# Three of eight column chunks of x transposed by VectorE blocks and a round trip through DRAM, in a one-core hybrid encoder layer

## The chip, the core and the metric

The kernel runs on one core of one Trainium2 chip. The core has five engines, each working through its own queue in order: TensorE (PE in the profile; its weight loads are PEld), VectorE (DVE), ScalarE (ACT), GpSimd (POOL) and SyncE (SP), which here only issues transfers. Transfers run on 16 DMA engines that all queues share. The metric is the device time of the core in microseconds (us), the median of several runs: 633.74 before the change (three runs, 633.61 to 633.91).

## The reference

One layer of a bidirectional hybrid encoder, 512 tokens by 2048 features, in float32: x is normalised, projected by w_in to q, k, v, two gates and an LRU input; attention and a gated linear recurrence run on their parts; both are normalised, gated, and projected by w_out onto x.

```python
def hybrid_layer(x, norm_w, w_in, ...):
    h = rms_norm(x, norm_w)
    proj = jnp.einsum('bsd,de->bse', h, w_in)
    q, k, v, g_attn, xr, g_lru = jnp.split(proj, SPLITS, axis=-1)
    attn_out = attention_group(q, k, v, q_norm_w, k_norm_w)
    lru_out = lru_group(xr, conv_w, conv_b, lru_wa, lru_ba, lru_wx, lru_bx, lru_lambda)
    mixed = jnp.concatenate([rms_norm(attn_out, attn_norm_w) * jax.nn.silu(g_attn),
                             rms_norm(lru_out, lru_norm_w) * jax.nn.silu(g_lru)], axis=-1)
    return x + jnp.einsum('bse,ed->bsd', mixed, w_out)
```

## The kernel before

Every matrix product is made of three products of split operands: a float32 value v is kept as a high part (v rounded to the fp32r type) and a low part (v minus the high part), and `mm3` (lines 151 to 154) multiplies high by high, low by high and high by low. So each operand costs a cast on ScalarE (the high) and a subtraction on VectorE (the low).

The program begins with the first half of the LRU input's projection, `proj_feat(C_XR, a1, ...)` (line 301): four accumulators `pj_162` to `pj_165` in PSUM, and eight chunks c = 0 to 7 of 256 input features each. Below, "x5" is chunk 5 of x and "w5" chunk 5 of w_in. For chunk c it needs

- the rows of w_in (512 KB), loaded by `wraw` into a ring of three buffers `wr`, split by `wsplit` (lines 216 and 217) into `wh` and `wl`, of which there are two chunks' worth;
- 256 columns of x for all 512 tokens (512 KB), loaded by `xload` (line 235) into a buffer `b`, with tokens on the partitions, and turned so that features lie on the partitions. `xturn` (line 238) does that on TensorE: for each half of the chunk four 128x128 transposes into PSUM (line 242), which ScalarE scales by norm_w into the high `xh` (line 244) and VectorE into the low `xl` (line 245), both named x in the profile;
- 24 matmuls (four accumulators, two halves, three products).

`xsquare` (line 249) adds up the squares of each token in the untransposed chunk. When all eight are in, `xstats` (line 293) makes 1/rms on GpSimd (`rstd`), puts it on two diagonals (line 284, `k_106` and `k_107` before, `k_109` and `k_110` after) and spreads it over the partitions by two matmuls (line 290) and a copy (`rbc`, line 291). The accumulators are multiplied by rbc when they are read out (line 395, `evac_bc`). The small vectors of the LRU (conv_w, biases, lambda, norms) are loaded in seven transfers into `vec_st` by `vec_load` (line 179), transposed once on TensorE by `columns` (line 188, the tile `mm_553` before, `mm_609` after) and copied into `vec` on VectorE (line 190). `lru_consts` (line 359) makes constants `lc` of vec in some 25 tiny VectorE steps.

What sets the order: TensorE runs in the order of the program text. SP does so until the end of this stage, ScalarE and VectorE until chunk 1's third accumulator (`s1`, `s2` in lines 1075 to 1080); after that a scheduler orders them by priority, with loads, splits and turns of x raised by `high_priority(AHEAD)`. In the compiled program each transfer of SP carries one of eight completion semaphores in turn, and waits until the transfer that had the same one before has landed.

In the last part of the program the attention already turns q and k without TensorE: `sent` (line 551) transposes 32x32 blocks on VectorE (line 559), writes the result to DRAM (`qd`, line 565), and `landed` (line 568) reads it back in four transfers that put each block in its place (`lq`, line 573); `moved` (line 643) does the same with the attention weights (`u`, `pd`, `pt`).

Of the kernel before, what the change touches and what calls it, by code (L numbers as in the profile page):

```python
# [17 lines left out]
P = 128  # L18
# [33 lines left out]
B = 32  # L52
NQ = P // B

# [8 lines left out]
def hybrid_kernel(  # L63
# [144 lines left out]
    turn_of = [0]  # L208

    def wsplit(raw, k, copy=nc.scalar.copy):  # L210
# [6 lines left out]
        nc.vector.tensor_sub(lo, raw[:, k, :], f(hi))  # L217
# [9 lines left out]
    ssq = const([P, NT, KT // 2], "ssq")  # L227

# [9 lines left out]
    def xturn(xc, kk):  # L238
# [5 lines left out]
        nc.scalar.activation(xh[kk], pt, AF.Identity, scale=nw[:, kk : kk + 1])  # L244
# [4 lines left out]
    def xsquare(xc, c):  # L249
        for t in range(NT):  # L250
            nc.vector.scalar_tensor_tensor(
                xc[:, t, :], xc[:, t, :], 1.0, xc[:, t, :], op0=ALU.mult, op1=ALU.mult,
                accum_out=ssq[:, t, c : c + 1],
            )

    def xchunk(c):
        with tc.high_priority(AHEAD):
            (xc,) = xload(c)
        yield
        with tc.high_priority(AHEAD):  # L260
            for k in range(2):
                xturn(xc, 2 * c + k)
        xsquare(xc, c)
# [287 lines left out]
    def sent(es, nh, *us):  # L551
# [5 lines left out]
        for n, u in enumerate(us):  # L557
            for t, e in enumerate(es):
                nc.vector.transpose(
                    u[:, :, :, t, :].rearrange("p b h r -> p h b r"),  # L560
                    e[:, 2 * n : 2 * n + 2].rearrange("p h (b c) -> p h b c", c=B),
                )
            aside_ = dram.tile([P, NQ, 2 * SEQ // NQ], F32, name=nm("qd"), tag="qd", bufs=5)
            yield
            nc.sync.dma_start(aside_, u.rearrange("p b h t r -> p b (h t r)"))
            asides.append(aside_)

    def landed(aside_):

        to = pools["qkv"].tile([P, NQ, 2, NT, B], F32, tag="lq", bufs=2, name=nm("lq"))  # L570
        src = aside_.rearrange("(i c) b x -> b c i x", c=B)
        for b in range(NQ):
            nc.sync.dma_start(
                to[b * B : (b + 1) * B].rearrange("p i h t r -> p i (h t r)"), src[b]
            )
        return to

    def split_head(pair, k, hi, lo):
        src = pair[:, :, k]
        hi, lo = (v.rearrange("p (t i r) -> p i t r", t=NT, i=NQ) for v in (hi, lo))  # L580
# [513 lines left out]
    loads, turns = iter(chunks), iter(chunks)  # L1094
    for step in proj_feat(C_XR, a1, first, given):
        if step is None:
# [4 lines left out]
            next(next(loads), None)  # L1101
# [232 lines left out]
```

## Time and profile before

| | |
|---|---|
| median of 3 runs | 633.74 us (633.61 to 633.91) |
| the profiled execution, its own time | 634.36 us |
| its span in the profile | 632.2 us |
| TensorE, VectorE, ScalarE, GpSimd busy | 99%, 78%, 54%, 17% of the span |
| mean DMA rate over the span | 197 GB/s |
| granted TensorE clock | 1.00 |

The profile is of one execution. Its timeline gives start and length of each instruction, with the tile it writes and those it reads; "[1.64 <-ACT x L244]" means that the engine stood idle for 1.64 us before it and that ScalarE's line 244 ended that. Matmuls are pipelined, so their lengths overlap (0.39 each) and the distance from start to start, 0.2275 in this stage, is what one costs. The other engines overlap a little too: a 128x512 subtraction on VectorE lasts 0.69 and the next starts after 0.60.

### The profile page before, as it was taken

What the parts mean: (1) busy time and instruction counts of PE and PEld (TensorE: products, weight loads), DVE (VectorE), ACT (ScalarE), POOL (GpSimd) and SP (SyncE); (2) the same over time, 40 slices, a digit from 0 to 9 for tenths busy, and PEclk for the clock granted to TensorE, in tenths of its full rate; (3) what the DMA queues carried; (4) which work ended last, traced back from release to release, by engine and by line L of the source; (5) the groups of instructions that cost most, each with busy time, mean ns of one, the idle gap of its engine ahead of it and who ended that gap; (6) DMA issues with size and microseconds to landing.
All of it is one profiled execution on the core that took longest, in us unless ns stands there. A gap on an engine that the chain in (4) does not pass through costs nothing.

```text
span 632.2 us, 8303 instructions
## 1 busy us (share of the span) xinstructions
PE 625.8 (99%) x2795; PEld 516.4 (82%) x2795; DVE 492.9 (78%) x808; ACT 341.6 (54%) x582; POOL 104.5 (17%) x137
## 2 busy tenths in 40 slices
PE   8999999999999999999999999999999999999997
PEld 6888888888888888888888888888888888888885
DVE  5789688986698875787787887549978866886885
ACT  3534799479936822645475547335445534443441
POOL 0010110212003532521123233100310001010010
PEclk9999999999999999999999999999999999999999
DMA  9844675768774599389659646923995676796152
GB/s 298 272 146 131 156 191 152 186 145 192 217 235 156 167 221 259 78 193 270 198 175 271 198 129 186 275 80 112 244 236 186 220 242 226 291 355 217 67 200 101
DMA packets 71436, 124.48 MB, mean 197 GB/s; under 512 B 6377, under 2 KB 27489, under 8 KB 71393
## 3 DMA queue, kind: packets, MB, share of 16 engines
q1 hardware_dynamic: 63360, 106.11, 53.1%
q0 software_dynamic: 7712, 17.31, 14.1%
q10 hardware_dynamic: 320, 0.53, 0.3%
q8 instruction: 22, 0.36, 0.2%
q14 instruction: 22, 0.17, 0.1%
HBM read 108.72 MB, written 36.18 MB: 229 GB/s over the span
## 4 chain that ended last, share of the span: by engine, by line
PE 98%; DMA 1%; ACT 0%; DVE 0%; ACTq 0%; DVEq 0%; issue 0%
PE pj L152 20%; PE pj L153 20%; PE pj L154 20%; PE mm L955 14%; PE pj L955 10%; PE mm L154 3%; PE mm L152 3%; PE mm L153 3%; DMA wr<-in_w_in_dram 1%; PE mm L242 1%; PE pj L310 0%; PE mm L749 0%; PE mm L290 0%; DVE cb L986 0%; ACT wh L216 0%; ACT x L244 0%
## 5 line engine op out<-in xcount | busy, mean ns | idle before, releaser
L152 PE MATMUL pj<-x,wh 128*128 128x512 f32 x376 | 147.2, 392 | 0.0
L153 PE MATMUL pj<-x,wh 128*128 128x512 f32 x376 | 146.6, 390 | 0.0
L154 PE MATMUL pj<-x,wl 128*128 128x512 f32 x376 | 146.4, 389 | 0.0
L216 ACT CAST wh<-wr 128x512 fp32r<-128x512 f32 x143 | 85.9, 618 | 104.4 <-PE pj L153 41.9
L217 DVE TENSOR_TENSOR wl<-wr,wh 128x512 fp32r<-128x512 f32 x144 | 100.4, 723 | 22.0 <-ACT wh L216 20.9
L807 ACT CAST wh<-wr 128x1024 fp32r<-128x1024 f32 (+1 forms) x72 | 60.7, 860 | 74.9 <-PE mm L955 37.7
L808 DVE TENSOR_TENSOR wl<-wr,wh 128x1024 fp32r<-128x1024 f32 (+1 forms) x72 | 68.7, 984 | 28.2 <-ACT wh L807 28.1
L153 PEld LDWEIGHTS pj<-x,wh 128*128 128x128 f32 x376 | 70.6, 188 | 14.9 <-DVE x L245 0.3
L154 PEld LDWEIGHTS pj<-x,wl 128*128 128x128 f32 x376 | 70.6, 188 | 14.9
L152 PEld LDWEIGHTS pj<-x,wh 128*128 128x128 f32 x376 | 70.6, 188 | 14.6
L152 PE MATMUL pj<-wh,x 128*128 128x512 f32 x192 | 74.8, 390 | 0.0
L154 PE MATMUL pj<-wh,x 128*128 128x512 f32 x192 | 74.7, 389 | 0.0
L153 PE MATMUL pj<-wl,x 128*128 128x512 f32 x192 | 74.7, 389 | 0.0
L831 POOL DMA_DIRECT2D t<-in_w_out_dram x40 | 33.7, 909 | 139.3 <-DMA t<-in_w_out_dram 95.5
L955 PE MATMUL mm<-wl,mh 128*128 128x512 f32 x128 | 49.8, 389 | 0.0
L955 PE MATMUL mm<-wh,ml 128*128 128x512 f32 x128 | 49.8, 389 | 0.0
L955 PE MATMUL mm<-wh,mh 128*128 128x512 f32 x128 | 49.8, 389 | 0.0
L153 PEld LDWEIGHTS pj<-wl,x 128*128 128x128 f32 x192 | 36.0, 188 | 7.5
L152 PEld LDWEIGHTS pj<-wh,x 128*128 128x128 f32 x192 | 36.0, 188 | 7.5
L154 PEld LDWEIGHTS pj<-wh,x 128*128 128x128 f32 x192 | 36.0, 188 | 7.5
L637 POOL TENSOR_SCALAR p<-p,sm 128x512 f32<-128x512 f32 x32 | 24.2, 759 | 90.2 <-DVE sm L636 90.2
L955 PE MATMUL pj<-wl,mh 128*128 128x512 f32 x96 | 37.4, 389 | 0.0
(203 smaller groups left out, 1032.1 us busy)
## 6 DMA issues: line engine op xcount, KB each, us to landing
wr<-in_w_in_dram SPq DMA_DIRECT2D x71, 512.0 KB, 4.5
wr<-in_w_out_dram SPq DMA_DIRECT2D x24, 512.0 KB, 5.1
t<-in_w_out_dram POOLq DMA_DIRECT2D x40, 256.0 KB, 7.1
wr<-t SPq DMA_DIRECT2D x40, 256.0 KB, 5.0
pd<-u SPq DMA_DIRECT2D x16, 512.0 KB, 3.4
pt<-pd SPq DMA_DIRECT2D x64, 128.0 KB, 4.0
t<-in_w_out_dram SPq DMA_DIRECT2D x24, 256.0 KB, 4.7
t<-t SPq DMA_DIRECT2D x16, 256.0 KB, 5.4
```

The costliest lines, as they stand in the source:

```text
L152: nc.tensor.matmul(acc, lh, rh, start=start, stop=False)
L153: nc.tensor.matmul(acc, lh, rl, start=False, stop=False)
L154: nc.tensor.matmul(acc, ll, rh, start=False, stop=stop)
L216: copy(hi, raw[:, k, :])
L217: nc.vector.tensor_sub(lo, raw[:, k, :], f(hi))
L242: nc.tensor.transpose(pt[:, t * P : (t + 1) * P], xc[:, t, ks], ident)
L637: last_pool[0] = nc.gpsimd.tensor_scalar(p, p, sm, 0.0, op0=ALU.mult, op1=ALU.add).ins
L807: nc.scalar.copy(hi[:, to], b)
L808: nc.vector.tensor_sub(lo[:, to], b, f(hi[:, to]))
L831: nc.gpsimd.dma_start(dst, src, accum_op=ALU.add)
L955: nc.tensor.matmul(dst[s], lh[:, ts_], rh, start=i == 0 and j == 0, stop=i == 7 and j == 2)
```

## The change

x0 to x4 are turned as before. x5, x6 and x7 (`TURNED = 5`) take another way: VectorE transposes the 32x32 blocks of the chunk in four instructions (`blocks`, into a tile `xu`), SP writes them to DRAM (`put_aside`, `xd`) and reads them back in four transfers of 128 KB that put the blocks in place (`bring_back`, into a second tile `xu`), ScalarE scales both halves by norm_w in place and casts the highs, and VectorE subtracts for the lows. So 24 transposes of TensorE, with the six scalings and six subtractions from PSUM behind them, go, and 12 block transposes, 3 writes, 12 reads, 6 scalings, 6 casts and 6 subtractions come.

The squares of x5 to x7 (12 instructions) move from VectorE to ScalarE. A table `moves` says at which accumulator step each load, split and turn is put into the program. Pins (`issue_after`) queue one instruction behind another on its engine: the blocks of x5 behind the lows of w2 and those of x6 and x7 behind those of w3, the squares behind x4's highs, the scalings behind the latest split, the statistics behind x7's last low. The loads of vec_st go from behind x5's load to behind the reads of x7, the transpose of vec_st from after chunk 5 to after chunk 6, and the loads of the rope tables (`rk`, `rq`) behind the last load of this stage.

```diff
@@ -50,6 +50,7 @@
 
 
 B = 32
+TURNED = 5
 NQ = P // B
 
 
...
@@ -205,7 +206,7 @@
             loads_done[queue] = queue.dma_start(raw[:, ks, :], src[:, ks, :]).ins
             yield raw
 
-    turn_of = [0]
+    turn_of, split_done = [0], {}
 
     def wsplit(raw, k, copy=nc.scalar.copy):
 
...
@@ -214,7 +215,8 @@
         hi = pool.tile([P, SEQ], F32R, tag="wh", bufs=4, name=nm("wh"))
         lo = pool.tile([P, SEQ], F32R, tag="wl", bufs=4, name=nm("wl"))
         copy(hi, raw[:, k, :])
-        nc.vector.tensor_sub(lo, raw[:, k, :], f(hi))
+        done = nc.vector.tensor_sub(lo, raw[:, k, :], f(hi)).ins
+        split_done[-1] = split_done[turn_of[0] - k] = done
         return hi, lo
 
     def wload(w, r0, c0):
...
@@ -225,6 +227,7 @@
 
     xh, xl = [None] * KT, [None] * KT
     ssq = const([P, NT, KT // 2], "ssq")
+    highs, x_lows = {}, []
 
     def xload(c, nk=1):
 
...
@@ -241,26 +244,84 @@
             ks = slice(kk % 2 * P, (kk % 2 + 1) * P)
             nc.tensor.transpose(pt[:, t * P : (t + 1) * P], xc[:, t, ks], ident)
         xh[kk], xl[kk] = x2(), x2()
-        nc.scalar.activation(xh[kk], pt, AF.Identity, scale=nw[:, kk : kk + 1])
+        after = split_done[-1] if kk > 3 else None
+        with tc.issue_after(after) if after else nullcontext():
+            highs[kk // 2] = nc.scalar.activation(
+                xh[kk], pt, AF.Identity, scale=nw[:, kk : kk + 1]
+            ).ins
         nc.vector.scalar_tensor_tensor(
             xl[kk], pt, nw[:, kk : kk + 1], f(xh[kk]), op0=ALU.mult, op1=ALU.subtract
         )
 
     def xsquare(xc, c):
         for t in range(NT):
+            if c >= TURNED:
+                nc.scalar.activation(
+                    xc[:, t, :], xc[:, t, :], AF.Square, accum_out=ssq[:, t, c : c + 1]
+                )
+                continue
             nc.vector.scalar_tensor_tensor(
                 xc[:, t, :], xc[:, t, :], 1.0, xc[:, t, :], op0=ALU.mult, op1=ALU.mult,
                 accum_out=ssq[:, t, c : c + 1],
             )
 
+    def blocks(u, t, src):
+
+        nc.vector.transpose(
+            u[:, :, :, t, :].rearrange("p b k r -> p k b r"),
+            src.rearrange("p (k b c) -> p k b c", k=2, c=B),
+        )
+
+    def put_aside(u, tag, bufs):
+
+        aside_ = dram.tile([P, NQ, 2 * SEQ // NQ], F32, name=nm(tag), tag=tag, bufs=bufs)
+        nc.sync.dma_start(aside_, u.rearrange("p b k t r -> p b (k t r)"))
+        return aside_
+
+    def bring_back(to, aside_):
+
+        src = aside_.rearrange("(i c) b x -> b c i x", c=B)
+        for b in range(NQ):
+            nc.sync.dma_start(
+                to[b * B : (b + 1) * B].rearrange("p i k t r -> p i (k t r)"), src[b]
+            )
+
+    def in_order(v):
+        return v.rearrange("p (t i r) -> p i t r", t=NT, i=NQ)
+
     def xchunk(c):
         with tc.high_priority(AHEAD):
             (xc,) = xload(c)
         yield
+        if c < TURNED:
+            with tc.high_priority(AHEAD):
+                for k in range(2):
+                    xturn(xc, 2 * c + k)
+            xsquare(xc, c)
+            yield
+            return
+        u, back = (
+            ring.tile([P, NQ, 2, NT, B], F32, name=nm("xu")) for ring in (aring, hring)
+        )
+        with tc.high_priority(AHEAD), tc.issue_after(split_done[2 if c == TURNED else 3]):
+            for t in range(NT):
+                blocks(u, t, xc[:, t, :])
+            there = put_aside(u, "xd", KT // 2 - TURNED)
+        with tc.issue_after(highs[TURNED - 1]):
+            xsquare(xc, c)
+        yield
         with tc.high_priority(AHEAD):
+            bring_back(back, there)
+        yield
+        with tc.high_priority(AHEAD), tc.issue_after(split_done[-1]):
             for k in range(2):
-                xturn(xc, 2 * c + k)
-        xsquare(xc, c)
+                kk = 2 * c + k
+                xh[kk], xl[kk] = x2(), x2()
+                hi, lo = (in_order(v) for v in (xh[kk], xl[kk]))
+                v = back[:, :, k]
+                nc.scalar.activation(v, v, AF.Identity, scale=nw[:, kk : kk + 1])
+                nc.scalar.copy(hi, v)
+                x_lows.append(nc.vector.tensor_sub(lo, v, f(hi)).ins)
         yield
 
     last_pool = [None]
...
@@ -494,7 +555,8 @@
     def rope_consts():
         rq, rk = (pools["rope"].tile([P, NT, 2, HD], F32, name=n, tag=n) for n in ("rq", "rk"))
         for dst, src, sc in ((rk, k_norm_w, 1.0), (rq, q_norm_w, HD**-0.5)):
-            nc.sync.dma_start(dst, rope.rearrange("(t p) c d -> p t c d", p=P))
+            with tc.issue_after(last_x):
+                nc.sync.dma_start(dst, rope.rearrange("(t p) c d -> p t c d", p=P))
             wb = k2(shape=(P, 2, HD))
             nc.sync.dma_start(wb[:, 0, :], src[None, :].broadcast_to([P, HD]))
             if sc != 1.0:
...
@@ -1091,33 +1144,58 @@
         xturn(xc, 0)
         busy(WARM2)
     chunks = [xchunk(c) for c in range(1, KT // 2)]
-    loads, turns = iter(chunks), iter(chunks)
+
+    raws = {}
+
+    def fetch_x(c):
+        with tc.high_priority(AHEAD):
+            (raws[c],) = wraw(w_in, c * 2 * P, C_XR)
+
+    def split_x(c):
+        with tc.high_priority(AHEAD):
+            given[c] = [wsplit(raws[c], k) for k in range(2)]
+
+    moves = {
+        None: "x1", (0, 2): "x1",
+        (1, 0): "x2", (1, 1): "x2", (1, 2): "x3 w2 s2", (1, 3): "x3",
+        (2, 0): "x4 x5", (2, 1): "x4 w3", (2, 2): "x6 x7", (2, 3): "w4 s3",
+        (3, 0): "x5 w5 x5", (3, 1): "x6 x7", (3, 3): "s4 x5",
+        (4, 0): "w6 x6 x7", (4, 3): "s5 x6",
+        (5, 0): "w7", (5, 3): "s6 x7", (6, 3): "s7",
+    }
+
+    def move(step):
+        for name in moves.get(step, "").split():
+            n = int(name[1])
+            if name[0] == "x":
+                next(chunks[n - 1])
+            else:
+                (fetch_x if name[0] == "w" else split_x)(n)
+
     for step in proj_feat(C_XR, a1, first, given):
         if step is None:
             with tc.high_priority():
                 first.append(wsplit(raw, 1))
                 xturn(xc, 1)
             xsquare(xc, 0)
-            next(next(loads), None)
+            move(None)
             given[1] = wload(w_in, 2 * P, C_XR)
             continue
         c, e = step
-        if (e == 0 or e == 2) and c:
-            next(next(loads, iter(())), None)
-        if (e, c) == (2, 0) or (e == 1 and c) or (e, c) in ((3, 1), (3, 2)):
-            next(next(turns, iter(())), None)
+        move(step)
         if (c, e) == (1, 2):
-            given[2] = wload(w_in, 4 * P, C_XR)
             s2.close()
-        if (c, e) == (2, 3):
-            vec_load()
-        if (c, e) == (5, 3):
+        if (c, e) == (4, 2):
+            with tc.high_priority(AHEAD):
+                vec_load()
+        if (c, e) == (6, 3):
             columns(vec, vec_st)
         if (c, e) == (KT // 2 - 1, 0):
-            with tc.high_priority():
+            with tc.high_priority(), tc.issue_after(x_lows[-1]):
                 xstats()
 
     s1.close()
+    last_x = loads_done[nc.sync]
     lru_consts()
     fill = proj_feat(C_XR + SEQ, a2)
     wsums = itertools.chain(first_sums(), more_sums())
```

The hunk left out lets `sent` and `landed` call the same new helpers; what they do is unchanged.

Three places of the compiled order, as they stand before and now. First SP, from x5's load (`b_57` before) and w4's load (`wr_380` now) on. Before:

```order
L235 DMA b_57_366<-in_x_dram 128x4x256
L179 DMA vec_st<-in_conv_w_dram 32x128
L179 DMA vec_st<-in_conv_b_dram 8x128
L179 DMA vec_st<-in_lru_ba_dram 16x128
L179 DMA vec_st<-in_lru_bx_dram 16x128
L179 DMA vec_st<-in_lru_lambda_dram 16x128
L179 DMA vec_st<-in_attn_norm_w_dram 8x128
L179 DMA vec_st<-in_lru_norm_w_dram 8x128
L205 DMA wr_403<-in_w_in_dram 128x2x512
L235 DMA b_69_419<-in_x_dram 128x4x256
L235 DMA b_76_455<-in_x_dram 128x4x256
L205 DMA wr_463<-in_w_in_dram 128x2x512
```

Now (w3, `wr_362`, x6 and x7 stand right before this, behind x5):

```order
L206 DMA wr_380<-in_w_in_dram 128x2x512
L278 DMA xd_402<-xu_396 128x1024
L206 DMA wr_408<-in_w_in_dram 128x2x512
L285 DMA xu_397<-xd_402 32x4x256 x4
L278 DMA xd_426<-xu_420 128x1024
L278 DMA xd_438<-xu_432 128x1024
L206 DMA wr_480<-in_w_in_dram 128x2x512
L285 DMA xu_421<-xd_426 32x4x256 x4
L285 DMA xu_433<-xd_438 32x4x256 x4
L180 DMA vec_st<-in_conv_w_dram 32x128
```

`wr_403` and `wr_362` are w3, `wr_463` and `wr_380` w4, `wr_408` w5, `wr_480` w6; `xd_402`, `xd_426` and `xd_438` are x5, x6 and x7 in DRAM. vec_st has moved from ahead of w3 to behind x7's reads; w7 (`wr_539`) comes right after the seventh of its loads.

Then VectorE in the middle of the stage, from the lows of w2 (`wl_288`, `wl_292`) on. Before:

```order
L217 TENSOR_TENSOR wl_288<-wr_285,wh_287 128x512
L217 TENSOR_TENSOR wl_292<-wr_285,wh_291 128x512
L245 SCALAR_TENSOR_TENSOR x_46_308<-mm_302,nw,x_45_307 128x512
L245 SCALAR_TENSOR_TENSOR x_49_317<-mm_311,nw,x_48_316 128x512
L217 TENSOR_TENSOR wl_406<-wr_403,wh_405 128x512
L217 TENSOR_TENSOR wl_410<-wr_403,wh_409 128x512
L251 SCALAR_TENSOR_TENSOR b_38_283,ssq<-b_38_283 128x256 x3
L245 SCALAR_TENSOR_TENSOR x_53_344<-mm_338,nw,x_52_343 128x512
L245 SCALAR_TENSOR_TENSOR x_56_353<-mm_347,nw,x_55_352 128x512
L251 SCALAR_TENSOR_TENSOR b_38_283,ssq<-b_38_283 128x256
```

Now:

```order
L218 TENSOR_TENSOR wl_288<-wr_285,wh_287 128x512
L218 TENSOR_TENSOR wl_292<-wr_285,wh_291 128x512
L252 SCALAR_TENSOR_TENSOR x_46_308<-mm_302,nw,x_45_307 128x512
L252 SCALAR_TENSOR_TENSOR x_49_317<-mm_311,nw,x_48_316 128x512
L218 TENSOR_TENSOR wl_383<-wr_362,wh_382 128x512
L218 TENSOR_TENSOR wl_387<-wr_362,wh_386 128x512
L270 STREAM_TRANSPOSE xu_396<-b_51_332 128x2x4x32 x3
L252 SCALAR_TENSOR_TENSOR x_54_346<-mm_340,nw,x_53_345 128x512
L252 SCALAR_TENSOR_TENSOR x_57_355<-mm_349,nw,x_56_354 128x512
L270 STREAM_TRANSPOSE xu_396<-b_51_332 128x2x4x32
```

`wl_406`, `wl_410` before and `wl_383`, `wl_387` now are the lows of w3; the pairs of line 245 (now 252) are the lows of x3 and x4. Where squares of x3 stood, the block transposes of x5 (`xu_396`) stand, and then those of x6.

Last VectorE at the end of the stage, around the copy of vec. Before:

```order
L295 TENSOR_REDUCE xsum<-ssq 128x4
L217 TENSOR_TENSOR wl_563<-wr_556,wh_562 128x512
L281 CAST part_610<-rstd 128x4
L282 TENSOR_TENSOR part_611<-rstd,part_610 128x4
L284 TENSOR_TENSOR k_106_612<-ident,part_610 128x512
L284 TENSOR_TENSOR k_107_613<-ident,part_611 128x512
L217 TENSOR_TENSOR wl_593<-wr_590,wh_592 128x512
L190 COPY vec<-mm_553 128x104
L217 TENSOR_TENSOR wl_597<-wr_590,wh_596 128x512
L364 TENSOR_SCALAR lc_641<-vec 128x16
L365 TENSOR_TENSOR lc_641<-lc_641,vec 128x16
```

Now:

```order
L356 TENSOR_REDUCE xsum<-ssq 128x4
L342 CAST part_622<-rstd 128x4
L343 TENSOR_TENSOR part_623<-rstd,part_622 128x4
L345 TENSOR_TENSOR k_109_624<-ident,part_622 128x512
L191 COPY vec<-mm_609 128x104
L345 TENSOR_TENSOR k_110_625<-ident,part_623 128x512
L425 TENSOR_SCALAR lc_653<-vec 128x16
L426 TENSOR_TENSOR lc_653<-lc_653,vec 128x16
L218 TENSOR_TENSOR wl_602<-wr_539,wh_601 128x512
L218 TENSOR_TENSOR wl_606<-wr_539,wh_605 128x512
L428 TENSOR_SCALAR lc_655<-lc_654 128x16
L438 TENSOR_SCALAR lc_653<-vec 128x16
```

`wl_593` and `wl_597` before and `wl_602` and `wl_606` now are the lows of w7. Before, they stood on both sides of the copy, and the copy's transpose `mm_553` was one chunk further ahead on TensorE. Now they stand behind the copy, the second diagonal `k_110` and two steps of `lc`. On TensorE `mm_609` stands between chunk 6's last matmul and chunk 7's first, and chunk 7's third matmul reads `wl_602`.

More of the change, by code (lines that the diff above doesn't have):

```diff
@@ L1 @@
 import itertools
-from contextlib import ExitStack
+from contextlib import ExitStack, nullcontext
 import numpy as np
@@ L558, in sent @@
             for t, e in enumerate(es):
[L559 to L563, printed above, removed]
+                blocks(u, t, e[:, 2 * n : 2 * n + 2].rearrange("p h d -> p (h d)"))
             yield
-            nc.sync.dma_start(aside_, u.rearrange("p b h t r -> p b (h t r)"))
-            asides.append(aside_)
+            asides.append(put_aside(u, "qd", 5))
     def landed(aside_):
         to = pools["qkv"].tile([P, NQ, 2, NT, B], F32, tag="lq", bufs=2, name=nm("lq"))
[L571 to L575, printed above, removed]
+        bring_back(to, aside_)
         return to
@@ L579, in split_head @@
         src = pair[:, :, k]
-        hi, lo = (v.rearrange("p (t i r) -> p i t r", t=NT, i=NQ) for v in (hi, lo))
+        hi, lo = (in_order(v) for v in (hi, lo))
         nc.scalar.copy(hi, src)
```

## The prediction

> **What bounds the kernel now.** I read the page first (part 1, then part 4, the chain that ended last), then a table of busy time by stage, then the timelines of the first 60 us, where the whole change lies.
>
> ```profile
> span 632.2 us, 8303 instructions
> PE 625.8 (99%) x2795; PEld 516.4 (82%) x2795; DVE 492.9 (78%) x808; ACT 341.6 (54%) x582; POOL 104.5 (17%) x137
> PE 98%; DMA 1%; ACT 0%; DVE 0%; ACTq 0%; DVEq 0%; issue 0%
> 12.60:60.00 47.40, 47.40 (x234) 39.38 (x233) 39.94 (x127) 19.25 (x32) 1.60 (x2) 1.00 0.59 191
> L242 PE MATMUL mm<-ident,b 128*128 128x128 f32 x64 | 8.5, 273 | 0.0
> ```
>
> TensorE is the bound, alone: 98% of the chain, and from 12.6 to 60 us it is busy for 47.40 of 47.40 us at a granted clock of 1.00. VectorE has 39.94 of the 47.40, ScalarE only 19.25. So a TensorE instruction taken out is worth its full pitch, and any new wait of TensorE costs its full length. The last row is what the change attacks: 64 transposes of x, of which chunks 5 to 7 have 24.
>
> **The gain.** Each chunk's eight transposes stand between two projection matmuls:
>
> ```profile
> 27.05 0.39 PE L154 MATMUL pj<-x,wl 128*128 128x512 f32 x1
> 27.28 1.03 PE L242 MATMUL mm<-ident,b 128*128 128x128 f32 x8
> 28.07 0.48 PE L152 MATMUL pj<-x,wh 128*128 128x512 f32 x1
> 28.38 0.40 PE L153 MATMUL pj<-x,wh 128*128 128x512 f32 x1
> ```
>
> Start to start, 27.05 to 28.38 is 1.33 us for what would be two matmul pitches of 0.2275: 0.875 us for eight transposes. Three chunks: **-2.63 us**. TensorE reaches 27.28 unchanged; without the transposes a chunk of 24 matmuls takes 24 x 0.2275 = 5.46 us, so chunk 3 starts at 27.28, chunk 5 at 38.2, chunk 6 at 43.66, and the transpose of vec_st, now ahead of chunk 7, comes at 49.12.
>
> **The new round trip, chunk 5.** Its start hangs on VectorE's queue:
>
> ```profile
> GB/s 0 230 308 376 380 352 366 358 320 41 121 274 370 261 365 369 377 274 289 12 0 0 259 50 39 351 303 232 256 19 0 187 112 5 30 336 214 34 241 183
> 18.21 1.14 ACT L216 CAST wh<-wr 128x512 fp32r<-128x512 f32 x2
> 21.65 1.14 ACT L216 CAST wh<-wr 128x512 fp32r<-128x512 f32 x2 [2.30 <-DMA wr<-in_w_in_dram]
> 20.48 1.29 DVE L217 TENSOR_TENSOR wl<-wr,wh 128x512 fp32r<-128x512 f32 x2
> 23.41 1.41 DVE L245 SCALAR_TENSOR_TENSOR x<-mm,nw,x 128x512 fp32r<-128x512 f32 x2 [1.64 <-ACT x L244]
> 227.63 2.07 DVE L559 STREAM_TRANSPOSE uq<-ev 128x256 f32<-128x256 f32 x6
> ```
>
> The first row (40 slices of the first 70 us) shows the DMA engines full to 15.75 us and nearly still after. The seven vec_st loads now leave, w3, x6, x7 and w4 follow x5 at once, and at 0.52 MB over 360 GB/s = 1.46 us each w3 lands near 18.5 instead of 21.65. ScalarE's highs of w3 then follow those of w2 (from 18.21), x3's highs come right behind, and VectorE's lows of x3 start at 21.7 instead of 23.41. After them by the order printed: two lows of w3 (1.2), three block transposes (2.07 for six, so 0.34 each), two lows of x4 (1.3), the fourth block transpose: done at 27.0. Then write, four reads and the split:
>
> ```profile
> pd<-u SPq DMA_DIRECT2D x16, 512.0 KB, 3.4
> pt<-pd SPq DMA_DIRECT2D x64, 128.0 KB, 4.0
> DMA to landing us min/median/max: 3.2/4.0/7.4
> 285.60 2.18 SPq L653 DMA_DIRECT2D pt<-pd  x4
> L244 ACT ACTIVATE x<-mm,nw x16: 680/682/690, 5.0 to 38.4; 128x512 fp32r<-128x512 f32 x16
> L581 ACT CAST q<-lq x8: 617/621/627, 266.4 to 360.6; 128x512 fp32r<-128x512 f32 x8
> L582 DVE TENSOR_TENSOR q<-lq,q x8: 648/680/684, 269.7 to 361.5; 128x512 fp32r<-128x512 f32 x8
> ```
>
> Write 3.4, the fourth read issued 1.6 later (three quarters of 2.18), landing 4.0: 27.0 + 9.0 = 36.0 by medians; with the fastest read (3.2) 35.2. Then two scalings of about 0.6 pitch, a cast of 0.62 and the subtraction 0.68, since ScalarE scales both halves before it casts: first low 2.6 us after landing, 38.6 or 37.8, against TensorE's second matmul of chunk 5 at 38.4. **Chunk 5 costs 0 to 0.2.** The 12 squares that move from VectorE to ScalarE cost nothing: ScalarE has 28 of the 47 us free, they are done under TensorE's chunks 2 to 4, and at most 0.62 each (a cast twice as wide) they take 7.4; without that cover those 7.4 would push chunk 5's scalings.
>
> **Chunks 6 and 7** queue behind that on SP: the reads of chunk 5 block the writes of 6 and 7, since SP runs in order; w6 waits there too, to 33.4, lands by 38 and is due at 43.66. By the same rows: writes at 32.6 and 33.0, the first landed at 36.2, reads issued to 38.2, landed at 41.4 to 42. The limit for chunk 6 is 43.9 - 2.6 = 41.3: 0.1 to 0.7 late. Chunk 7's reads follow to 40.5 and land near 43.5; its limit is about 46.5, but the statistics now hang on its lows (below). I take **+0.4** for all three chunks together, bounds 0 and 3.8.
>
> **The wait that the order itself makes.** This is the dearest new thing, and no transfer is part of it. VectorE now has, in a row: the first diagonal k_109, the copy of vec, the second diagonal, two steps of lc, and only then the lows of w7. The copy of vec needs the transpose mm_609, which on TensorE stands right before chunk 7, and chunk 7's third matmul needs the first of those lows. In the kernel before, the lows of w7 stood around a copy that came a whole chunk earlier:
>
> ```profile
> 46.28 0.25 PE L188 MATMUL mm<-ident,vec_st 104*128 104x104 f32 x1
> 46.31 0.48 PE L152 MATMUL pj<-x,wh 128*128 128x512 f32 x1
> 46.85 0.40 PE L154 MATMUL pj<-x,wl 128*128 128x512 f32 x1
> 43.67 1.29 DVE L284 TENSOR_TENSOR k<-ident,part 128x512 fp32r<-128x512 f32 x2
> 46.22 0.69 DVE L217 TENSOR_TENSOR wl<-wr,wh 128x512 fp32r<-128x512 f32 x1 [1.26 <-ACT wh L216]
> 46.83 0.26 DVE L190 COPY vec<-mm 128x104 f32<-128x104 f32 x1
> 47.01 0.68 DVE L217 TENSOR_TENSOR wl<-wr,wh 128x512 fp32r<-128x512 f32 x1
> 47.61 0.17 DVE L364 TENSOR_SCALAR lc<-vec 128x16 f32<-128x16 f32 x1
> 47.81 0.17 DVE L365 TENSOR_TENSOR lc<-lc,vec 128x16 f32<-128x16 f32 x1
> 52.20 0.17 DVE L374 TENSOR_SCALAR lc<-lc 128x16 f32<-128x16 f32 x1
> 52.31 0.69 DVE L217 TENSOR_TENSOR wl<-wr,wh 128x512 fp32r<-128x512 f32 x1
> 5.62 0.43 DVE L216 CAST wh<-wr 128x512 fp32r<-128x512 f32 x1 [0.99 <-DMA wr<-in_w_in_dram]
> 6.20 1.18 PE L310 MATMUL pj<-x,wh 128*128 128x512 f32 x4 [0.64 <-DVE wh L216]
> ```
>
> From the start of the small transpose: 0.25 for itself, 0.18 for the copy (46.83 to 47.01), 0.60 for the second diagonal (1.29 for two), 0.20 (47.61 to 47.81), 0.11 (52.20 to 52.31), 0.69 for the low itself, and 0.15 until a matmul that waits for new weights starts (5.62 + 0.43 to 6.20): 2.18. Without a wait the third matmul starts 46.85 - 46.28 = 0.57 after. **+1.6 us**, bounds 1.4 and 2.0 while VectorE is free at 49.4. Queued behind on VectorE are the second lows of w7 (0.6 later, needed 0.68 later), the lows for the next projection and rbc, all due at 54 or later, so nothing else is late.
>
> It is free at 49.4 if chunk 7's data has landed by 43.3:
>
> ```profile
> 41.39 0.18 DVE L295 TENSOR_REDUCE xsum<-ssq 128x4 f32<-128x32 f32 x1
> 43.39 0.17 DVE L281 CAST part<-rstd 128x4 fp32r<-128x4 f32 x1 [1.22 <-POOL rstd L271]
> ```
>
> The sum of squares is pinned behind chunk 7's last low (3.1 after landing), GpSimd's rstd takes 2.0 and the diagonal 0.9: 6.0 after landing. At 43.5 that is 0.1 late, within the 0.4.
>
> **Hidden.** w7's load is issued when chunk 7's last read has landed (its semaphore lane) and takes 4.5 more: near 48, its highs at 48.6, due at 49.1. rk and rq move from 21 us to where the rope constants are built; their 1 MB costs nothing while SP's w loads keep two chunks ahead. The later order on VectorE shifts by a few rows; the evacuations and lows that TensorE waits for keep 0.3 us or more.
>
> **Sum.** The profiled execution took 634.36 (span 632.2 and 2.16 around it), 0.62 over the median 633.74. 634.36 - 2.63 + 1.6 + 0.4 = 633.7 for it, and on the median's scale 633.74 - 0.63 = **633.1**.
>
> **Rivals.** (1) *The whole gain*: 631.1. For it: TensorE never waited in this stretch before, and the round trip fits by the fastest rows. Against it: the copy of vec cannot run before its transpose and engines run in order, so only a wrong reading of the order gives this. Chance 0.17.
>
> (2) *The round trip is late, slower than before.* Rows of transfers that met others:
>
> ```profile
> qd<-uq SPq DMA_DIRECT2D x2, 512.0 KB, 6.9
> lq<-qd SPq DMA_DIRECT2D x6, 128.0 KB, 8.7
> ```
>
> The writes of chunks 6 and 7 go out as such a pair, behind chunk 5's reads and ahead of w6. At 6.9 instead of 3.4 to 3.6 chunk 6's reads land at 45.1, 3.8 past the limit: 633.74 - 2.63 + 1.6 + 3.8 = 636.5. It decides from 2.3 us of lateness on (635.0). Against it: those rows fall where GpSimd's adds load the DMA too, and here only SP sends. Chance 0.17. The Trainium skill (DMA: Bandwidth & Descriptors, Anatomy of one DMA) speaks of a delay that can be surprisingly long when the target is HBM, yet fits a fixed 2.0 us plus bytes over 436 GB/s. By that fit, an estimate, the write takes 3.2 and a read 2.3, chunk 5 lands at 34.1 and this rival is dead; the medians above, 3.4 and 4.0, agree with it for the write and not for the read.
>
> (3) *vec_st is late.* mm_609 waits for all seven small loads, whose last is issued when chunk 7's third read has landed, about 43.2:
>
> ```profile
> DMA to landing us min/median/max: 5.0/6.0/8.6
> ```
>
> That is their landing in the kernel before, behind nine loads of 0.25 to 0.5 MB. At 6.0 they land at 49.2, on time; at 8.6 at 51.8, 2.7 late: 633.74 - 2.63 + 1.6 + 2.7 = 635.4. Here the queue ahead of them is short. Chance 0.09.
>
> **How the numbers follow.** The forecast has 0.57, its own range 632.2 to 634.3. The bound of 0.2% is 1.27 us: faster is under 632.47, slower over 635.01. Faster: rival 1 and the forecast's low edge, 0.17 + 0.08 = 0.25. Slower: most of rivals 2 and 3, 0.13 + 0.05 = 0.18. Same: 0.57. The range 631.0 to 635.5 leaves out the upper part of rivals 2 and 3.
>
> **What would show it.** 40 transposes of 128x128 instead of 64 and TensorE's busy time 2.6 lower, or near it; one wait of TensorE near 49.7 for VectorE's wl of about 1.6; xu's four block transposes ended near 27.0; chunk 5's reads landed between 35 and 36, chunk 6's between 40.5 and 42. Wrong if no wait stands before chunk 7's third matmul, or if TensorE waits over 1 us for an x of chunks 5 to 7, or anywhere after 60 us.

## The result and the profile after

The changed kernel takes **636.94 us** (median of 8 runs, 634.76 to 638.22) against 633.93 for the kernel before on the same chip (8 runs, 633.61 to 634.31): 1.0045 times as long, 95% interval 1.0032 to 1.0058. It is 3.0 us slower, outside the predicted 631.0 to 635.5. Its runs also spread over 3.5 us, where those of the kernel before spread over 0.7.

The profiled execution took 636.34 us with a span of 634.2. The page's part 1:

```profile
PE 624.2 (98%) x2771; PEld 513.5 (81%) x2771; DVE 491.7 (78%) x796; ACT 348.6 (55%) x612; POOL 104.4 (16%) x137
```

The table of busy time by stage (the stretch, its length, then TensorE's busy time):

```profile
12.60:60.00 47.40, 45.41 (x211) 36.80 (x210) 35.81 (x95) 26.34 (x61) 1.24 (x2) 1.00 0.80 246
60.00:120.00 60.00, 58.78 (x260) 48.35 (x259) 51.14 (x90) 49.12 (x74) 6.89 (x8) 1.00 0.72 184
120.00:500.00 380.00, 380.00 (x1681) 313.88 (x1680) 298.24 (x471) 215.72 (x404) 84.21 (x101) 1.00 0.70 192
500.00:632.00 132.00, 129.00 (x568) 105.98 (x566) 100.30 (x127) 51.60 (x66) 11.00 (x18) 1.00 0.64 215
```

And the transposes of x on TensorE, by their line (count, then ns, first and last start):

```profile
L245 PE MATMUL mm<-ident,b x40: 270/272/329, 4.4 to 23.7; 128*128 128x128 f32 x40
```

TensorE has 24 transposes fewer, but it is no longer busy without a gap: it stands for 1.99 us before 60 us and for 1.22 between 60 and 120, where it had none. Its busy time is 1.6 us lower (624.2 against 625.8), where the prediction's sign was 2.6; a matmul behind a wait counts as busy for longer (0.50 us instead of 0.39 at 51.59), which is part of the difference. All its waits, the longest first (who waited, for whom, total, times, longest):

```profile
PE pj L155 <- DVE wl L218: 1.4, 1, 1.4
PE mm L153 <- ACT b L508: 1.2, 1, 1.2
PE mm L1124 <- POOL ones L161: 1.1, 1, 1.1
PE pj L1008 <- DVE cb L1039: 0.6, 1, 0.6
PE pj L371 <- DVE wh L217: 0.4, 1, 0.4
PE pj L153 <- ACT x L323: 0.4, 1, 0.4
PE pj L154 <- DVE x L324: 0.2, 1, 0.2
```

The third and fifth, at the very start, the kernel before had too (1.1 and 0.64). In order of time the new ones are x of chunk 6 (0.40 and 0.23 at 43.4 and 44.2), w7's lows at 51.59, the gate products of the recurrence at 98.02, and an accumulator bank of the last stage at 557.23.

**Where the time went.** For every TensorE instruction that both kernels have, I take its start in a profile minus its start in the profile before, and read how that difference grows by stretch (stretches by the times of the kernel before; minus is gained):

| us | to 10.8 | 10.8 to 52.4 | 52.4 to 100 | 100 to 540 | 540 to 556 | to the end | sum |
|---|---|---|---|---|---|---|---|
| the changed kernel | -0.57 | -0.06 | +1.54 | +0.01 | +0.96 | +0.01 | +1.89 |
| e1, the same kernel again | +0.22 | +0.43 | +0.78 | +0.04 | +1.55 | +0.32 | +3.34 |
| e2, lows first | -0.25 | -0.83 | +0.30 | 0.00 | +0.87 | 0.00 | +0.09 |
| e3, pairs | -0.01 | -0.58 | +0.04 | -0.02 | +0.89 | +0.41 | +0.73 |
| e4, both | -0.23 | -0.81 | +0.71 | +0.01 | +1.24 | -0.01 | +0.91 |
| e5, e2 with 24 more warm-ups | -0.25 | -0.73 | +0.02 | +0.01 | +0.96 | 0.00 | +0.01 |
| e6, e4 with early norms | -0.09 | -1.36 | -0.02 | +0.02 | +0.66 | +0.02 | -0.77 |
| e7, e6 with 24 more warm-ups | +0.28 | -0.50 | +0.04 | +0.02 | +0.19 | +0.01 | +0.04 |
| e8, e6 with later residual | -0.24 | -1.27 | 0.00 | +0.02 | +0.19 | +0.05 | -1.25 |
| e9, e8 with lows before diagonals | -0.23 | -1.02 | +0.15 | +0.02 | 0.00 | 0.00 | -1.08 |
| e10, kernel before, later residual | -0.21 | -0.16 | 0.00 | -0.02 | -0.01 | -0.01 | -0.41 |

The first column is the first loads' landing, which varies by up to 0.6 us either way and has nothing to do with the edits (e10's -0.21 is the kernel before). Some 0.17 of the second column is a slow spot near 14 us in the one profile before: e10, the kernel before again, does without it, and so do all runs but e1 and e8. The rest says that the first stage, the only place that the change was meant for, comes out about even; the loss lies in two places far behind it, at 98 and at 557 us.

**98 us.** ScalarE, SP and TensorE there, first of the changed kernel, then of the kernel before (start, length, engine, line, output<-input, idle time before it and its releaser):

```profile
88.16 3.05 SPq L466 DMA_DIRECT2D k<-in_lru_wa_dram  x4
91.25 2.00 SPq L467 DMA_DIRECT2D k<-in_lru_wx_dram  x4
96.76 0.62 ACT L481 CAST k<-k 128x512 fp32r<-128x512 f32 x1 [2.35 <-DMA k<-in_lru_wx_dram]
98.02 0.50 PE L153 MATMUL mm<-k,k 128*128 128x512 f32 x1 [1.22 <-ACT b L508]
```

```profile
88.47 0.38 SPq L405 DMA_DIRECT2D k<-in_lru_wa_dram  x1
88.90 0.46 SPq L406 DMA_DIRECT2D k<-in_lru_wx_dram  x1
93.81 0.62 ACT L420 CAST k<-k 128x512 fp32r<-128x512 f32 x1
97.24 0.39 PE L152 MATMUL mm<-k,k 128*128 128x512 f32 x1
```

The gate weights of a block come in two halves, wa and wx, and the cast of the high needs both. In the kernel before the scheduler let the first block's pair go first, 88.47 and 88.90. In the changed kernel it issues all four wa and only then the wx: 91.25 for the first. The cast waits 2.35 us, and the sigmoids behind it on ScalarE, which empty TensorE's PSUM banks, wait with it.

**557 us.** VectorE in the changed kernel, the adds of the residual x onto the finished accumulators (L1084), then TensorE; and VectorE in the kernel before:

```profile
539.84 1.23 DVE L1084 TENSOR_TENSOR xt<-xt,wr 128x1024 f32<-128x1024 f32 x1 [2.15 <-DMA wr<-in_x_dram]
540.98 1.82 DVE L861 TENSOR_TENSOR wl<-wr,wh 128x1024 fp32r<-128x1024 f32 x2
544.11 1.22 DVE L1084 TENSOR_TENSOR cb<-cb,wr 128x1024 f32<-128x1024 f32 x1 [1.31 <-DMA wr<-in_x_dram]
557.23 0.47 PE L1008 MATMUL pj<-wh,mh 128*128 128x512 f32 x1 [0.57 <-DVE cb L1039]
```

```profile
539.55 1.23 DVE L1031 TENSOR_TENSOR xt<-xt,wr 128x1024 f32<-128x1024 f32 x1 [2.78 <-DMA wr<-in_x_dram]
540.69 1.82 DVE L808 TENSOR_TENSOR wl<-wr,wh 128x1024 fp32r<-128x1024 f32 x2
542.43 1.22 DVE L1031 TENSOR_TENSOR cb<-cb,wr 128x1024 f32<-128x1024 f32 x1
```

VectorE stands once for x in the kernel before (2.78 us) and twice now (2.15 and 1.31, 3.46 in all). Its evacuation of the bank (L1039) then comes 0.57 us too late, though no edit touches this code.

### The profile page after: what moved, and what is told of

It reads as the page before. It is cut to its first block, busy times and chain, and to the rows that moved or that the text cites. A ratio compares the mean times of both kernels' runs of the same rounds, so it can differ in the third digit from the quotient of the medians.

```text
span 634.2 us, 8303 instructions
## 1 busy us (share of the span) xinstructions
PE 624.2 (98%) x2771; PEld 513.5 (81%) x2771; DVE 491.7 (78%) x796; ACT 348.6 (55%) x612; POOL 104.4 (16%) x137
## 4 chain that ended last, share of the span: by engine, by line
PE 89%; DMA 6%; DVE 2%; SPq 2%; issue 1%; ACT 0%; ACTq 0%; DVEq 0%
PE pj L155 19%; PE pj L153 19%; PE pj L154 19%; PE mm L1008 11%; PE pj L1008 9%; PE mm L153 3%; PE mm L155 3%; PE mm L154 3%; DMA wr<-in_w_out_dram 2%; DMA k<-in_lru_wx_dram 1%; DMA xd<-xu 1%; DVE wl L861 1%; PE pj L371 1%; DMA xu<-xd 1%; DMA wr<-in_w_in_dram 1%; PE mm L245 1%
## 5 line engine op out<-in xcount | busy, mean ns | idle before, releaser
L1008 PE MATMUL pj<-wh,mh 128*128 128x512 f32 x96 | 37.4, 390 | 0.6 <-DVE cb L1039 0.6
```

Source lines behind the costliest of these rows:

```text
L1008: nc.tensor.matmul(dst[s], lh[:, ts_], rh, start=i == 0 and j == 0, stop=i == 7 and j == 2)
```

## The experiments

All are timed against the kernel before on the same chip; e1 to e4, e5 to e7 and e8 to e10 ran together, the last three on another chip. "The gates" are the products near 98 us, "the last stage" is the stretch from 540 to 556 us of the table above.

| | median (range), runs | before | ratio, 95% interval |
|---|---|---|---|
| e1 | 637.0 (635.18 to 637.96), 6 | 634.05 | 1.0042, 1.0028 to 1.0055 |
| e2 | 634.05 (632.74 to 637.27), 12 | 634.05 | 1.0005, 0.9993 to 1.0016 |
| e3 | 635.11 (634.37 to 637.0), 12 | 634.05 | 1.0017, 1.0009 to 1.0026 |
| e4 | 634.6 (633.45 to 636.0), 11 | 634.05 | 1.001, 1.0001 to 1.0018 |
| e5 | 634.78 (633.64 to 638.86), 12 | 634.23 | 1.0018, 1.0003 to 1.0032 |
| e6 | 634.19 (632.79 to 635.24), 11 | 634.23 | 1.0, 0.9991 to 1.0008 |
| e7 | 633.76 (632.89 to 635.06), 11 | 634.23 | 0.9991, 0.9982 to 1.0 |
| e8 | 633.73 (632.73 to 634.45), 11 | 634.2 | 0.999, 0.9981 to 0.9999 |
| e9 | **632.86** (631.65 to 634.93), 11 | 634.2 | 0.9977, 0.9967 to 0.9987 |
| e10 | 634.04 (633.69 to 634.86), 11 | 634.2 | 0.9998, 0.9989 to 1.0007 |

**e1: the changed kernel again.**

> The changed kernel once more, for a second profile. Theory A (two fixed waits made by instruction order): TensorE again waits about 1.2 to 1.5 us near 51.6 us for VectorE's wl and about 1.0 to 1.4 us near 98 us for ScalarE's b (behind the cast that waits for the lru_wx load); the wait of 0.6 us in the last stage near 557 us may come or go. Time 636.2 to 637.5. Theory B (the extra time is transfers that land late in some executions): one of the first two waits is under 0.4 us here.

The wait for w7's lows is there to the hundredth (1.37); the one at the gates is 0.4 and came down because the first wx took 4.7 us to land instead of 5.5; the last stage lost more. The time, 637.0, is as theory A has it. By its letter A holds for the first wait (1.4) and fails for the second (0.44), and B just misses its 0.4: the order makes the gate wait possible, the landing decides its size.

```profile
97.27 0.62 ACT L481 CAST k<-k 128x512 fp32r<-128x512 f32 x1 [1.57 <-DMA k<-in_lru_wx_dram]
98.53 0.50 PE L153 MATMUL mm<-k,k 128*128 128x512 f32 x1 [0.44 <-ACT b L508]
```

**e2: w7's lows ahead of the copy of vec.**

```diff
         if (c, e) == (6, 3):
-            columns(vec, vec_st)
+            with tc.issue_after(split_done[-1]):
+                columns(vec, vec_st)
```

> VectorE's copy of vec is put behind the lows of w7. Theory A: the wait near 51.6 us goes (under 0.2 us left), nothing else changes, 1.3 to 1.6 us faster than the changed kernel. Rival: TensorE arrives earlier at the gate products near 98 us, whose data come by the clock of the lru loads, and the 1.4 us come back there as a longer wait (2.5 us or more): time within 0.4 us of the changed kernel.

```profile
49.20 1.28 DVE L345 TENSOR_TENSOR k<-ident,part 128x512 fp32r<-128x512 f32 x2
50.40 1.28 DVE L218 TENSOR_TENSOR wl<-wr,wh 128x512 fp32r<-128x512 f32 x2
51.61 0.26 DVE L191 COPY vec<-mm 128x104 f32<-128x104 f32 x1
51.14 0.50 PE L155 MATMUL pj<-x,wl 128*128 128x512 f32 x1 [0.47 <-DVE wl L218]
```

The wait falls from 1.37 to 0.47, and not under 0.2 as expected: the copy of vec and the tiny steps are behind the lows now, but both diagonals are still ahead. The median is 2.95 under e1's, where the wait became only 0.90 shorter and 1.3 to 1.6 were expected. In this profile the gates cost 0.30 instead of 1.54 (the cast waited 0.82), and only 2 of 12 runs are over 636 us, against 7 of 8 and 4 of 6 of the changed kernel. The rival, that the time comes back at the gates, did not happen. Why the gate loads land sooner when TensorE is 0.9 us ahead was not settled.

**e3: each block's gate loads as a pair**, the same loads in another order on SP:

```diff
+            with tc.high_priority(AHEAD), tc.issue_after(pair) if pair else nullcontext():
                 nc.sync.dma_start(gr[:, 0:2, :], lru_wa[:, n].rearrange("d c e -> c d e"))
-                nc.sync.dma_start(gr[:, 2:4, :], lru_wx[:, n].rearrange("d c e -> c d e"))
+                wx = nc.sync.dma_start(gr[:, 2:4, :], lru_wx[:, n].rearrange("d c e -> c d e"))
+            pair = wx.ins if half else None
```

> In the second half of the recurrent gates each block's lru_wa and lru_wx loads are issued next to each other, as the first block's were in the kernel before. Theory A (the wait near 98 us comes from the first block's lru_wx being the fifth of eight loads): the cast of that block's gate weights no longer waits for a DMA, TensorE's wait near 98 us goes, 1.0 to 1.4 us faster than the changed kernel. Rival (the transfers there are slow, whatever their order): the cast still waits over 1 us and the time stays within 0.4 us.

```profile
88.46 0.37 SPq L466 DMA_DIRECT2D k<-in_lru_wa_dram  x1
88.88 0.47 SPq L467 DMA_DIRECT2D k<-in_lru_wx_dram  x1
94.30 0.62 ACT L482 CAST k<-k 128x512 fp32r<-128x512 f32 x1 [0.42 <-DMA k<-in_lru_wx_dram]
```

The issue is back at 88.88 and TensorE's wait at 98 us is gone (0.04 in that stretch); the median is 1.9 under e1's (1.0 to 1.4 expected). The cast still waits 0.42, because the load takes 5.3 us, where the kernel before had its weights after at most 4.9. So by this run the order of the eight loads has a part in that wait. It is not the whole cause: e4 below has this order and loses time at the gates, and e5 has the order of the changed kernel and loses 0.02.

**e4: e2 and e3 together.**

> Both edits. Theory A: both waits gone, the two gains add up to 2.4 to 3.0 us: 633.9 to 634.6, the time of the kernel before. What is left of the 2.6 us of transposes would then have been lost after 98 us. Rival (the early time is absorbed at a later wait set by transfers): less than 1.6 us faster than the changed kernel, with a longer wait near 557 us.

The gains don't add: 2.4 in all, 0.55 less than e2 alone. The time, 634.6, is at the edge of theory A's range, but the waits are not gone: the first block's wx is issued at 88.76 here but lands 6.0 us later, the gates cost 0.71 again, and 0.5 is left at w7. No run is over 636 us.

Over the profiles so far and e5's, TensorE's loss at the gates follows the cast's wait in either order. In the order of the changed kernel a wait of 2.35 us cost 1.54, 1.57 cost 0.78 (e1), 0.82 cost 0.30 (e2) and 0.53 cost 0.02 (e5); in pairs 1.14 cost 0.71 (e4) and 0.42 cost 0.04 (e3).

```profile
94.82 0.62 ACT L482 CAST k<-k 128x512 fp32r<-128x512 f32 x1 [1.14 <-DMA k<-in_lru_wx_dram]
96.08 0.50 PE L153 MATMUL mm<-k,k 128*128 128x512 f32 x1 [0.39 <-ACT b L509]
```

**e5: is it the instruction stream?** The transfers of instructions have queues of their own in the trace. In the changed kernels one of 16 KB (q8) falls into the end of the burst of loads and output writes at 530 to 545 us; in the kernel before it falls earlier. Three microseconds of each, of the kernel before from 531, of e2 from 537 (queue: packets, MB, share of 16 engines; 2.3% of 16 engines for 3 us is 1.1 us of one engine):

```profile
q8 instruction: 1, 0.02, 1.8%
```

```profile
q8 instruction: 1, 0.02, 2.3%
```

e5 is e2 with `busy(WARM + 24, 92)` in place of `busy(WARM)`: 38 warm-up matmuls of 92 columns instead of 14 of 256, which put the 24 missing matmuls back ahead of everything.

> As e2_lows_first, with 24 more warm-up matmuls before the first load has landed (38 of 92 columns instead of 14 of 256, about as long together), so that TensorE has again as many instructions ahead of each place as in the kernel before. Theory C (the wait near 555 us comes from where TensorE's instruction stream is fetched: the 16 KB fetch on queue q8 that fell at 529 to 532 us before now falls at 538 to 541 us, into the end of the burst of loads and output writes there, and delays x's load): the q8 packet is back near 531 us, VectorE's wait for x before cb's residual falls from 1.6 us to 0.5 or less, TensorE's wait for cb goes, 0.7 to 0.9 us faster than e2_lows_first: 633.0 to 633.5. Rival (the burst is late for another reason, or lane numbers decide): the wait of 0.6 us for cb stays and the time is within 0.3 us of e2_lows_first.

The packet went where the theory said (528 to 531 us; so q8 carries TensorE's instructions), and it changed which x is late:

```profile
539.04 1.23 DVE L1084 TENSOR_TENSOR xt<-xt,wr 128x1024 f32<-128x1024 f32 x1 [3.22 <-DMA wr<-in_x_dram]
542.23 1.23 DVE L1084 TENSOR_TENSOR cb<-cb,wr 128x1024 f32<-128x1024 f32 x1 [0.23 <-DMA wr<-in_x_dram]
```

Against e2 (2.05 and 1.59) the second wait is nearly gone and the first is 1.2 longer. The sum fell by 0.2 only, TensorE's wait stayed at 0.6, and the time did not fall; 3 of 12 runs are over 636 us. The rival's wait is right and its time, within 0.3 us of e2, is not.

All twelve profiles side by side say more. The rows are the start of the q8 packet, the time from issue to landing of the x for xt and of the x for cb, VectorE's two waits for them added up, and the last stage's loss:

| | before | e10 | e7 | e5 | e6 | changed | e2 | e3 | e4 | e1 | e8 | e9 |
|---|---|---|---|---|---|---|---|---|---|---|---|---|
| q8 packet at | 531.8 | 531.7 | 531.9 | 530.6 | 538.4 | 541.1 | 539.3 | 539.4 | 539.3 | 541.6 | 538.5 | 539.9 |
| x for xt took | 8.2 | 7.9 | 8.1 | 8.6 | 7.5 | 7.5 | 7.4 | 7.6 | 7.6 | 7.5 | 7.5 | 7.4 |
| x for cb took | 8.0 | 7.8 | 8.0 | 8.9 | 8.6 | 8.9 | 9.1 | 9.1 | 9.5 | 9.5 | 8.5 | 9.1 |
| VectorE waits | 2.78 | 0 | 2.76 | 3.45 | 3.14 | 3.46 | 3.64 | 3.67 | 4.02 | 4.04 | 0 | 0 |
| last stage loses | - | -0.01 | 0.19 | 0.96 | 0.66 | 0.96 | 0.87 | 0.89 | 1.24 | 1.55 | 0.19 | 0 |

TensorE's loss follows VectorE's waits: 0.19 at most up to 2.78 us, 0.66 at 3.14, 0.87 and more from 3.45 on. And the fetch goes with which x is slow: with the packet before 532 us the first takes 7.9 to 8.6 and the second, but for e5, 8.0 or less; with the packet from 538 on they take 7.4 to 7.6 and 8.5 to 9.5. So C names something real. That it sets the kernel's time is not shown: in e7 the same edit took the last stage's loss from 0.66 to 0.19, but in e5 the second x is slow all the same, and the time did not fall.

**e6: the norm weights in tiles of their own**, loaded early, so that the gate loads need not wait for a buffer that VectorE frees only after rk's products:

```diff
-            wb = k2(shape=(P, 2, HD))
-            nc.sync.dma_start(wb[:, 0, :], src[None, :].broadcast_to([P, HD]))
+            wb = const([P, 2, HD], nm("wb"))
+            with tc.issue_after(last_x):
+                nc.sync.dma_start(wb[:, 0, :], src[None, :].broadcast_to([P, HD]))
```

(with the products of rk and rq pinned behind the split before them, and the edits of e4.)

> As e4_both, with k_norm and q_norm kept in tiles of their own and loaded behind the last w of the first projection, so that the first block's lru_wa and lru_wx need not wait for rk's products on VectorE and are issued some 6 us earlier. Theory: the cast of the second half's gate weights waits for no DMA, TensorE's wait near 98 us is 0.1 us or less in the profile, and the time is 0.3 to 0.7 us under e4_both's: 633.9 to 634.3, with a smaller spread. The wait near 555 us stays at about 0.6. Rival (that wait is not from the lru loads): 0.4 us or more stays at 98 us.

```profile
92.97 0.62 ACT L482 CAST k<-k 128x512 fp32r<-128x512 f32 x1
```

The cast waits for nothing and that stretch costs -0.02. That and the time are as expected; the first block's loads go out at 80.70 and 85.61 instead of e4's 88.34 and 88.76. The spread is as wide as e4's (2.5 us), but the highest run is 635.24. In e6 to e9, which all have this edit, the stretch costs 0.15 at most and none of 44 runs is over 635.3.

**e7: all of it, with the warm-ups of e5.**

> All edits together: lows of w7 first, pairs, early norms, the 24 warm-up matmuls. Theories A and C: 1.1 us ahead at 52 us, nothing lost at 98 us, nothing at 555 us: 632.7 to 633.2, 0.9 to 1.3 us faster than the kernel before. If C falls: 633.7 to 634.2.

633.76 is in the range for "C falls". In the profile it was not the last stage, which lost 0.19, but chunk 6's x, which was 0.8 late.

**e8: the residual one step later.** The last two adds of x get two more lows ahead of them on VectorE:

```diff
-                        if 2 <= i < 6:
-                            next(rs[i - 2])
-                            if i < 4:
-                                next(rs[i])
+                        if i in (2, 3):
+                            next(rs[i - 2])
+                            next(rs[i])
+                        elif i in (5 - g, 6 - g):
+                            next(rs[i - 3 + g])
```

> As e6_gate_early, with the last two adds of x's residual in the first half of the last stage one step later on VectorE (two more lows ahead of each). Theory D (the wait near 555 us is VectorE standing in order before an add whose x has not landed, with the lows and the evacuations of the next banks queued behind it, wherever the burst's delay comes from): VectorE's waits for x at 537 to 542 us go, TensorE's wait for cb near 555 us goes, 0.5 to 0.8 us faster than e6_gate_early: 633.4 to 633.7. Rival (the lows themselves are late there because their w_out loads land late): the wait for cb stays at 0.4 or more, time within 0.3 us of e6.

```profile
539.28 1.22 DVE L1089 TENSOR_TENSOR xt<-xt,wr 128x1024 f32<-128x1024 f32 x1
544.69 1.22 DVE L1089 TENSOR_TENSOR cb<-cb,wr 128x1024 f32<-128x1024 f32 x1
```

No wait for x and no wait of TensorE for cb, though both x took as long as in e6 (7.5 and 8.5 us): the mechanism of D holds. What delayed the bank was VectorE standing in order before an add that was not urgent. What it is worth in time is less sure: 633.73 is 0.46 under e6's median, a little less than expected, but the two ran on different chips and their intervals against the kernel before overlap.

**e9: w7's lows ahead of the diagonals too.** `rows(rbc, ...)` pinned behind `split_done[-1]`, `columns(vec, vec_st)` and the next low behind the second diagonal.

> As e8, with the lows of w7 ahead of the statistics' diagonals too, and the copy of vec behind them. Theory A: the 0.5 us that TensorE still waits near 51 us in e2 to e7 go, 0.4 to 0.5 us faster than e8; with D 632.9 to 633.3, under the kernel before by 0.9 to 1.3 us. Rival: the diagonals are then late for the product with ones, and the same time is lost there.

```profile
48.66 1.29 DVE L219 TENSOR_TENSOR wl<-wr,wh 128x512 fp32r<-128x512 f32 x2 [0.51 <-ACT wh L217]
50.15 1.29 DVE L348 TENSOR_TENSOR k<-ident,part 128x512 fp32r<-128x512 f32 x2
51.99 0.62 PE L354 MATMUL mm<-k,ones_r 128*128 128x512 f32 x2
```

No wait is left at w7, and the product with ones follows without a gap, so the rival did not happen. 632.86 is 0.87 under e8 (0.4 to 0.5 expected), beats the kernel before by 0.23% (0.13 to 0.33) and lies 4.1 us under the changed kernel's median on the other chip. Its own remaining loss is chunk 6's x, 1.15 late in this profile.

**e10: the kernel before with e8's edit.**

> The kernel before with the same two adds one step later: what the edit of e8 is worth without the change. Its TensorE has no wait there, so both theories expect no gain: within 0.3 us of the kernel before (633.8 to 634.5).

634.04 against 634.2, nothing: that edit repairs a wait that only the change brings out.

## Why the prediction was wrong

- **The gain** of 2.63 was right: at each of the three places where eight transposes stood TensorE's start moves forward by 0.88 us against the kernel before, 2.65 in all, in all ten profiles with the change.
- **The round trip** was forecast at +0.4, and that term was too small. Its steps: xu's blocks ended near 26.2 (27.0 forecast), the write took 2.9 (3.4), chunk 5's x was there at 33.6 (35 to 36), chunk 6's at 41.5 (40.5 to 42). So chunk 5 was early and cost nothing. Chunk 6 cost 1.04 in the changed kernel, 1.34 in e1, and from 0.41 (e3) to 1.78 (e9) in the ten profiles, read as the growth of the difference from chunk 5's second matmul to chunk 6's third. That its landing fell into the forecast range is luck. TensorE was 0.8 us ahead of the forecast (chunk 6's first matmul was due at 42.87, not 43.66) and the reads went out 2.1 us earlier than forecast, but they took 5.2 us, not the 4.0 of the row; chunk 5's had taken 2.9. From the blocks' end to chunk 5's landing it took 7.4 us, where the medians of the rows gave 9.0. The fit that the prediction quoted from the Trainium skill (DMA: Bandwidth & Descriptors, Anatomy of one DMA), which the page gives for transfers that GpSimd issues, gave 34.1 less 27.0, an estimate of 7.1. That was nearer in the sum, but its read of 2.3 was too short for both chunks. Rival 2 did not happen.

```profile
26.24 2.91 DMA xd<-xu
33.63 1.34 ACT L322 ACTIVATE xu<-xu,nw 128x512 f32<-128x512 f32 x2 [0.99 <-DMA xu<-xd]
41.53 1.34 ACT L322 ACTIVATE xu<-xu,nw 128x512 f32<-128x512 f32 x2 [0.98 <-DMA xu<-xd]
```

The reads of chunk 5 (issued from 28 to 31 us) and of chunk 6 (from 34 to 36.3), with the median from issue to landing:

```profile
xu<-xd SPq DMA_DIRECT2D x4, 128.0 KB, 2.9
xu<-xd SPq DMA_DIRECT2D x4, 128.0 KB, 5.2
```

- **The wait that the order makes** was forecast at +1.6 near 49.7 for wl, and was that: 1.37 idle, 1.73 with the slower start behind it and the small transpose, for the reason given. So rival 1 did not happen.

```profile
49.49 0.25 PE L189 MATMUL mm<-ident,vec_st 104*128 104x104 f32 x1
50.85 1.29 DVE L218 TENSOR_TENSOR wl<-wr,wh 128x512 fp32r<-128x512 f32 x2
51.59 0.50 PE L155 MATMUL pj<-x,wl 128*128 128x512 f32 x1 [1.37 <-DVE wl L218]
```

vec_st was on time (49.49), so rival 3 did not happen either.

- **The step that failed is "Hidden"**: "The later order on VectorE shifts by a few rows; the evacuations and lows that TensorE waits for keep 0.3 us or more." It priced everything behind 60 us at nothing, from VectorE's rows alone. The gate wait is not on VectorE: it comes from a gate load that lands late, two engines away from TensorE, and it cost 1.54 and 0.78 in the two profiles. Issuing that load earlier removed it (e6 to e9); SP's order of the eight loads has a part in it by e3, but does not decide it alone (e4, e5). In the last stage VectorE does stand in the way, but its margin was no 0.3 us: a sum of its waits of 2.78 us cost TensorE nothing in the kernel before and 3.14 cost 0.66 in e6; 0.96 and 1.55 were lost there in the two profiles. Together that is some 2.4 us, of which the sum had none; nor had any rival, so the upper end of the range, 635.5, knew only the first stage. The text's own condition, a wait of over 1 us anywhere after 60 us, is what came. The first stage adds the 0.6 and 0.9 us by which the round trip was undersized in the two profiles.

What stays open is why the gate load and the two x land when they do.

## What to carry to other kernels

When a change lets a scheduler run again, compare the order of *all* queues over the whole program, the transfers above all, and ask of each pair of rows that swapped what needs the later one: here a load that moved from second to fifth place left a thin margin to its landing, and the loss behind it was 0.02 to 1.54 us in four profiles. Where an engine works in order, work that is not urgent and waits for a transfer (a residual add, a copy of constants) belongs behind the urgent work, even where a profile shows no harm yet. A spread between runs that grows with an edit can point to a wait for a transfer: with the gate loads early no run was over 635.3 us, though spreads of 1.7 to 3.3 us stayed.

## What the hardware showed that was not expected

The first block's wx load of 128 KB took 3.8 to 6.0 us to land in seven executions (e5 3.8, e2 4.2, e1 4.7, e3 5.3, the changed kernel 5.5, e4 6.0, the kernel before at most 4.9), with a w_in load of 512 KB and one or two w_out loads of 256 KB issued shortly before it. It was the second of the eight gate loads in the kernel before, e3 and e4 and the fifth in the others, and neither place had the shorter times. The instruction stream seems to cost the data transfers something: taking 24 matmuls out moved TensorE's 16 KB fetch from about 531 to about 539 us, and putting 24 short ones in at the start moved it back. In twelve executions the x for xt took 7.9 to 8.6 us with the early fetch and 7.4 to 7.6 with the late one, and the x for cb mostly the other way round. The Trainium skill (Runtime: NRT & Kernel Launch, Instruction fetch mechanics) has these fetches as 16 KiB blocks on a DMA queue of the sequencer's own, their cost mostly hidden. The block size agrees with the packets here (22 of them, 0.36 MB, in the kernel before), and TensorE indeed shows no wait for an instruction (it is busy for 380.00 of the 380 us from 120 to 500). In these executions it is a data transfer beside the fetch, not TensorE, that is slower.
